# RMSNorm and matmul on one core: the loads of x move from SyncE's DMA queue to ScalarE's

## The chip, the cores and the metric

The kernel runs on one core of a Trainium2 chip. A core has five engines with instruction streams of their own: TensorE (PE, matrix products), VectorE (DVE), ScalarE (ACT), GpSimd (POOL) and SyncE (SP), which computes nothing here and issues transfers. Transfers between device memory and the core's SBUF are carried out by 16 DMA engines. SyncE and ScalarE each have a DMA queue; what one of them issues goes through its queue. The metric is the device time of one execution in microseconds (us), given as the median of many runs.

## The reference

x has 16 x 1024 rows (tokens) of 512 numbers, the weight is 512 x 768, all float32. Each row is divided by its root mean square, multiplied by gamma and then by the weight:

```
rms = sqrt(mean(x ** 2, axis=-1) + eps)
out = (x / rms * gamma) @ weight          # 16 x 1024 x 768, float32
```

## The kernel before

The 16384 rows are 128 tiles of 128 rows. Dividing by the rms commutes with the product, so the kernel multiplies the raw rows, in bfloat16, with a weight into which gamma has been folded once, and scales each row of the result by 1/rms while it leaves PSUM.

One step `j` of the main loop (lines 301 to 326) handles a pair of tiles, 2j and 2j + 1. The order of the instructions on each engine is the order of the program text; nothing reorders it. For a tile:

- A load brings x into a buffer of 16 tiles (`xt`, `xin` with two buffers, 32 KB per partition each). `load_until(2 * j + AHEAD)` with `AHEAD = 20` (line 302) issues the load of the next 16 tiles at the top of iterations 7, 15, 23, 31, 39 and 47 (tiles 32, 48, 64, 80, 96, 112). The first 16 tiles come as loads of 2, 2, 4 and 8 tiles; tiles 16 to 31 as one load of 16, all issued before the loop (lines 234 to 237), with the weights between.
- GpSimd casts x to bfloat16 (`xb`, line 94, a pair at a time, three pairs ahead). TensorE transposes it against an identity matrix (line 133) two pairs ahead, woven between the matmuls by `feeder`; VectorE copies the transposes out of PSUM (`xT`, line 140). The last four tiles of each 16 from tile 28 on are cast four at a time (`cast_quad`, line 158) and transposed by VectorE in blocks (line 172) instead.
- ScalarE squares x and sums each row (line 98, two pairs ahead), takes the root for four tiles at once (line 102); VectorE inverts it (line 104).
- TensorE makes eight matmuls (line 194) into one of three PSUM accumulators (`ops`). `finish_tile` scales the result into an output buffer: ScalarE for even tiles (line 176), VectorE for odd ones (line 178).
- The output buffer (`ot`) holds 8 tiles, and there are three of them. When 8 tiles are done, `store` (line 191) writes them out in one transfer of 3072 KB (two, two and four tiles, then four and four at the start, four and four at the end). A buffer is written again 24 tiles later, once its store has landed.

All loads of x and of the weights and all stores are issued by SyncE (lines 83, 191, 232), on one queue. So a load on that queue stands behind the stores issued before it. Four tiny transfers of a corner of x into an unused tile (`mark`, line 265) are issued at j = 30 and four more at j = 54. ScalarE issues one transfer, gamma, at the start (line 226).

In iteration j the order on ScalarE is: squares of tiles 2j + 4 and 2j + 5, in every second iteration a root, the scaling of tile 2j.

Of the kernel before, what the change touches and what calls it, by code (L numbers as in the profile page):

```python
# [18 lines left out]
def kernel(  # L19
# [8 lines left out]
    nc = tc.nc  # L28
    P = 128

    x = x.flatten_outer_dims()
    out = out.flatten_outer_dims()
# [4 lines left out]
    NP = NT // 2  # L37
    XG, OG = 16, 8
# [7 lines left out]
    def stretches(group, parts):  # L46
        first, size, i = {}, {}, 0
        for g in range(NT // group):
            for n in parts.get(g, [group]):
                for t in range(i, i + n):  # L50
                    first[t], size[t] = i, n
                i += n
        return first, size

    last = NT // OG - 1
    x_first, x_size = stretches(XG, {0: [2, 2, 4, 8]})
    o_first, o_size = stretches(OG, {0: [2, 2, 4], 1: [4, 4], last: [4, 4]})

    def rows(ap, i, n):
        base, t = x_first[i], x_size[i]  # L60
        return ap[base * P:(base + t) * P, :].rearrange("(p t) d -> p t d", t=t)[:, i - base:i - base + n, :]

    singles = ctx.enter_context(tc.tile_pool(name="singles", bufs=1))
# [11 lines left out]
    x_tiles, xb_tiles, tp_tiles, rstd_of, xT_tiles, o_tiles, norm_sums = {}, {}, {}, {}, {}, {}, {}  # L75

    def held(tiles, group, i, n=1):
        return tiles[i // group][:, i % group:i % group + n, :]

    def load(i):  # L80
        if i // XG not in x_tiles:
            x_tiles[i // XG] = xin.tile([P, XG, D], F32, name="xt")
        nc.sync.dma_start(out=held(x_tiles, XG, i, x_size[i]), in_=rows(x, i, x_size[i]))  # L83

    starts = [i for i in range(NT) if x_first[i] == i]

    def load_until(i):
        while starts and starts[0] < i:
            load(starts.pop(0))

    def cast(i, engine, n=1):
        if i // 2 not in xb_tiles:
            xb_tiles[i // 2] = xbp.tile([P, 2, D], BF16, name="xb")
        engine.tensor_copy(out=xb_tiles[i // 2][:, i % 2:i % 2 + n, :], in_=held(x_tiles, XG, i, n))  # L94
# [13 lines left out]
    def norms(i, n):  # L108
        ssq = stats.tile([P, 4], F32, name="ssq")
        for t in range(n):  # L110
            square(i + t, ssq[:, t:t + 1])
        root(i, n, ssq)
# [30 lines left out]
    def transpose_tile(i):  # L143
        for h in range(2):
            transpose_word(i // 2, i % 2, h)
        evac(i // 2, i % 2, 1)
# [6 lines left out]
    def quad_of(j):  # L153
        return j // 2 if (2 * j) % XG >= XG - 4 and 2 * j >= XG else None
# [14 lines left out]
    def move_quad(n):  # L169
        for _ in range(min(n, len(quad_moves))):  # L170
            dst, src = quad_moves.pop(0)
            nc.vector.transpose(out=dst, in_=src)  # L172

    def scale(engine, dst, src, r):
        if engine is nc.scalar:
            nc.scalar.mul(out=dst, in_=src, mul=r)  # L176
        else:
            nc.vector.tensor_single_scalar(out=dst, in_=src, scalar=r, op=mybir.AluOpType.mult)  # L178

    def accumulator():  # L180
        return opsum.tile([P, 2, WIDE], F32, name="ops").rearrange("p a b -> p (a b)")
# [16 lines left out]
    def matmuls(i, acc, ks, feed=None):  # L198
        for k in ks:
            matmul(i, k, acc, 0, WIDE)  # L200
            if feed:
                feed()
            matmul(i, k, acc, WIDE, O)

    def finish_tile(i, acc, engine):
        scale(engine, out_tile(i), acc[:, :O], rstd_of[i])
        store(i)


    def feeder(pairs, gaps, alone=False):  # L210
        queue = [(j, t, h) for j in pairs for t in range(2) for h in range(2)]
        calls = iter(gaps)

        def feed():
            for _ in range(next(calls)):
                j, t, h = queue.pop(0)
                transpose_word(j, t, h)
                if alone and h == 1:
                    evac(j, t, 1)
                elif (t, h) == (1, 1):  # L220
                    evac(j)
        return feed

    with tc.manual_schedule():
        g_row = singles.tile([2, P, 2], F32)
        nc.scalar.dma_start(out=g_row, in_=gamma.rearrange("(h w c) -> h w c", w=P, c=2))
        nc.scalar.preload_act_table(AF.Sqrt)  # L227
        wv = weight.rearrange("(h w c) o -> w h (c o)", w=P, c=2)
        w_f32 = singles.tile([P, K, O], F32)

        def load_weights(h):
            nc.sync.dma_start(out=w_f32[:, 2 * h:2 * h + 2, :].rearrange("p c o -> p (c o)"), in_=wv[:, h, :])  # L232

        load_until(2)
        load_weights(0)
        load_weights(1)
        load_until(2 * XG)

        for _ in range(20):
            nc.sync.drain()  # L240


        warm = singles.tile([P, WIDE], BF16)
        nc.vector.memset(warm, 0.0)
        eps_sb = singles.tile([P, 1], F32)
        nc.vector.memset(eps_sb, float(eps))  # L246
        ident_f = singles.tile([P, P], F32)
        make_identity(nc, ident_f)
        spare = accumulator()

        def warm_up(n):
            for _ in range(n):
                nc.tensor.matmul(out=spare[:, :WIDE], lhsT=warm[:, :P], rhs=warm, start=True, stop=True)  # L253

        w_bf = singles.tile([P, K, O], BF16)

        def weights(k, engine, lo=0, hi=O):
            scale(engine, w_bf[:, k, lo:hi], w_f32[:, k, lo:hi], g_sb[:, k % 2, k // 2:k // 2 + 1])


        probe = singles.tile([16, 16 * 64], F32)

        def mark(counts):
            for k in counts:
                nc.sync.dma_start(out=probe[:k, 64 * k:64 * k + 4 * k], in_=x[:k, :4 * k])

        warm_up(6)
        gp = tpsum.tile([P, 2, 2], F32, name="tp")
        for c in range(2):
            nc.tensor.transpose(out=gp[:, c, :], in_=g_row[:, :, c], identity=ident_f[:2, :2])  # L270
        g_sb = singles.tile([P, 2, 2], F32)
        nc.vector.tensor_copy(out=g_sb, in_=gp)  # L272
        cast(0, nc.gpsimd)
        cast(1, nc.gpsimd)
        cast(2, nc.gpsimd, 2)
        norms(0, 2)
        warm_up(4)
        transpose_tile(0)
        transpose_tile(1)
        warm_up(2)  # L280
        weights(0, nc.vector, 0, WIDE)
        weights(0, nc.vector, WIDE, O)
        weights(1, nc.scalar)
        acc = [accumulator() for _ in range(2)]
        for i in range(2):
            matmuls(i, acc[i], [0, 1])
        weights(2, nc.vector)
        weights(3, nc.scalar)
        norms(2, 2)
        cast(4, nc.gpsimd)  # L290
        cast(5, nc.gpsimd)
        matmuls(0, acc[0], [2, 3])
        finish_tile(0, acc[0], nc.scalar)
        matmuls(1, acc[1], [2, 3], feeder([1], [2, 2], alone=True))
        finish_tile(1, acc[1], nc.vector)
        cast(6, nc.gpsimd, 2)

        mid, one, two, both = ([0, 0, 1, 1, 0, 1, 1, 0], [1, 1, 0, 1, 1, 0, 0, 0], [1, 0, 1, 0, 1, 0, 1, 0],
                               [1, 1, 1, 1, 1, 1, 1, 1])
        marks = {NP // 2 - 2: (8, 10, 12, 14), NP - 10: (7, 9, 11, 13)}  # L300
        for j in range(1, NP):
            load_until(2 * j + AHEAD)
            if j + 3 < NP and quad_of(j + 3) is None:
                cast(2 * j + 6, nc.gpsimd, 2)
            if (2 * j + 2) % XG == 0 and 2 * j + 2 < NT:
                cast_quad((2 * j + 2 + XG - 4) // 4)
            elif 2 * j >= XG:
                move_quad(3)
            if j < 4:
                norms(2 * j + 2, 2)  # L310
            if 3 <= j < NP - 2:
                norms_by_four(j + 2)
            if j in marks:
                mark(marks[j])
            if j < 3:
                feed = feeder([j + 1], mid if j == 1 else one, alone=j == 1)
            elif j == 3:
                feed = feeder([4, 5], both)
            elif j + 2 < NP and quad_of(j + 2) is None:
                feed = feeder([j + 2], two)  # L320
            else:
                feed = None
            for i, engine in ((2 * j, nc.scalar), (2 * j + 1, nc.vector)):
                a = accumulator()
                matmuls(i, a, range(K), feed)
                finish_tile(i, a, engine)
# [35 lines left out]
```

## Time and profile before

| | |
|---|---|
| median of 14 runs | 210.65 us (210.41 to 212.64) |
| profiled execution: its own time / span | 210.8 us / 208.9 us |
| TensorE busy | 193.5 us (93% of the span) |
| VectorE, ScalarE, GpSimd busy | 151.0, 149.6, 64.3 us |
| packets on SyncE's queue | 85.48 MB, 96.8% of the time of 16 DMA engines |
| store of 8 tiles: issue to landing | 16.3 us (median of 13 issues) |
| load of 16 tiles: issue to landing | 21.3 us |
| last store issued / landed | 200.54 / 207.9 us |

The profile is of one execution. Its span goes from the first to the last instruction; the time of a run is about 1.9 us longer. In groups of instructions a line such as "L94 POOL CAST xb<-xt" names the source line, the engine, the operation and what is written from what. In a timeline the columns are the start in us from the span's start, the duration in us, then engine, line and operation, and in brackets the idle time before it and what ended that. An engine name with a "q" (SPq) is its instruction sequencer, which issues transfers. In a row of windows the columns are the stretch, its length, then busy us of each engine with the number of instructions (PE, weight loads, DVE, ACT, POOL), the granted clock of TensorE as a share, the mean busy share of the DMA engines, and the GB/s that they moved.

### The profile page before, as it was taken

To read this page: it belongs to the slowest core of one execution; us is meant where nothing else is said; L and a number is where in the kernel's file an instruction comes from. 1 tells how busy PE (TensorE), PEld (TensorE's weight loads), DVE (VectorE), ACT (ScalarE), POOL (GpSimd) and SP (SyncE) were. 2 spreads that over 40 slices of the span, in tenths; PEclk is the share of its full clock that TensorE was granted. 3 is DMA by queue.
4 is the path that set the end of the run, shared out by engine and by line. 5 is a ranking of instruction groups with operands and counts; after the bars stand their busy time and mean duration, and the time that the engine had idled before them with its cause. 6 is when DMAs were issued, how large, how long until landed. Compare 5 with 4: busy or idle time off the path is not lost.

```text
span 208.9 us, 3443 instructions
## 1 busy us (share of the span) xinstructions
PE 193.5 (93%) x1214; PEld 129.6 (62%) x1238; DVE 151.0 (72%) x270; ACT 149.6 (72%) x358; POOL 64.3 (31%) x65
## 2 busy tenths in 40 slices
PE   7799969999999999999999999999999989999910
PEld 2467746676666667666667666776666657666500
DVE  0465635999579966999579966998589965999410
ACT  4698758778787787778787787778787778778310
POOL 3247059004810193005810086002920059000000
PEclk9999999999999999999999999999999999999995
DMA  6999999999999899999999999999999999995994
GB/s 236 428 441 471 336 389 433 474 403 420 431 439 414 353 447 452 414 419 431 424 442 425 434 420 433 449 430 417 420 442 425 423 430 442 413 414 231 449 409 202
DMA packets 4941, 85.69 MB, mean 410 GB/s; under 512 B 698, under 2 KB 700, under 8 KB 1468
## 3 DMA queue, kind: packets, MB, share of 16 engines
q1 hardware_dynamic: 4920, 85.48, 96.8%
q8 instruction: 9, 0.15, 0.3%
q14 instruction: 8, 0.07, 0.1%
q10 hardware_dynamic: 4, 0.00, 0.0%
HBM read 35.14 MB, written 50.33 MB: 409 GB/s over the span
## 4 chain that ended last, share of the span: by engine, by line
PE 67%; DMA 24%; SPq 1%; POOL 1%; ACT 1%; issue 1%; DVE 0%; POOLq 0%
PE ops L194 60%; DMA xt<-in_x_dram 24%; PE tp L133 8%; POOL xb L94 1%; SPq L83 1%; ACT jk L98 1%; DVE ot L178 0%; ACT ot L176 0%; SPq L232 0%; POOLq L94 0%
## 5 line engine op out<-in xcount | busy, mean ns | idle before, releaser
L194 PE MATMUL ops<-w_bf,xT 128*128 128x256 bf16 (+1 forms) x783 | 146.5, 325 | 1.4 <-DVE w_bf L178 0.6
L194 PEld LDWEIGHTS <-xT 128*128 128x128 bf16 x800 | 78.3, 98 | 46.3 <-issue 0.8
L176 ACT ACTIVATE ot<-ops,rstd 128x768 f32<-128x768 f32 x64 | 57.7, 901 | 42.3 <-PE ops L194 41.9
L94 POOL CAST xb<-xt 128x1024 bf16<-128x1024 f32 (+1 forms) x52 | 51.1, 1010 | 112.7 <-DMA xt<-in_x_dram 104.2
L98 ACT ACTIVATE jk<-xt 128x512 bf16<-128x512 f32 x128 | 78.8, 620 | 3.4 <-DMA xt<-in_x_dram 3.4
L178 DVE TENSOR_SCALAR ot<-ops,rstd 128x768 f32<-128x768 f32 x64 | 64.6, 1010 | 9.5 <-PE ops L194 9.0
L133 PE MATMUL tp<-ident_f,xb 128*128 128x128 f32 x200 | 54.0, 274 | 2.9 <-POOL xb L94 2.9
L140 DVE COPY xT<-tp 128x1024 bf16<-128x1024 bf16 (+1 forms) x53 | 34.7, 657 | 26.2 <-PE tp L133 25.5
L172 DVE STREAM_TRANSPOSE xTq<-xq 32x256 f32<-32x256 f32 x112 | 48.7, 435 | 1.9
L194 PE MATMUL ops<-w_bf,xTq 128*128 128x256 bf16 (+1 forms) x217 | 42.5, 324 | 0.4
L133 PEld LDWEIGHTS tp<-ident_f,xb 128*128 128x128 f32 x200 | 28.2, 142 | 7.1 <-POOL xb L94 4.7
L194 PEld LDWEIGHTS <-xTq 128*128 128x128 bf16 x224 | 22.0, 98 | 12.4
L98 ACT ACTIVATION_READ_ACCUMULATOR jk<-xt 128x1 f32 x128 | 24.4, 191 | 0.0
L158 POOL CAST xq<-xt 128x2048 bf16<-128x2048 f32 x7 | 13.3, 1897 | 0.0
L104 DVE RECIPROCAL rstd<-rms 128x4 f32<-128x4 f32 (+1 forms) x35 | 6.1, 176 | 7.6 <-ACT rms L102 6.9
L102 ACT ACTIVATE rms<-ssq,eps_sb 128x4 f32<-128x4 f32 (+1 forms) x35 | 10.4, 297 | 1.1
L253 PE MATMUL ops<-warm 128*128 128x512 bf16 x12 | 5.2, 587 | 1.2 <-DVE eps_sb L246 1.2
L253 PEld LDWEIGHTS <-warm 128*128 128x128 bf16 x12 | 1.4, 128 | 2.9 <-issue 1.7
L176 ACT ACTIVATE w_bf<-w_f,g_sb 128x768 bf16<-128x768 f32 x2 | 1.9, 936 | 1.2 <-DMA w_f<-in_weight_dram 1.2
L272 DVE COPY g_sb<-tp 128x4 f32<-128x4 f32 x1 | 0.2, 163 | 3.2 <-PE tp L270 3.2
L227 ACT ACT_TABLE_LOAD x1 | 1.3, 1283 | 1.3 <-PEq L343 1.3
L178 DVE TENSOR_SCALAR w_bf<-w_f,g_sb 128x512 bf16<-128x512 f32 (+2 forms) x3 | 1.4, 482 | 0.3 <-DMA w_f<-in_weight_dram 0.3
(10 smaller groups left out, 1.9 us busy)
## 6 DMA issues: line engine op xcount, KB each, us to landing
out_dram<-ot SPq DMA_DIRECT2D x13, 3072.0 KB, 16.3
xt<-in_x_dram SPq DMA_DIRECT2D x7, 4096.0 KB, 21.3
out_dram<-ot SPq DMA_DIRECT2D x5, 1536.0 KB, 7.4
xt<-in_x_dram SPq DMA_DIRECT2D x1, 2048.0 KB
w_f<-in_weight_dram SPq DMA_DIRECT2D x2, 768.0 KB
out_dram<-ot SPq DMA_DIRECT2D x2, 768.0 KB, 16.0
xt<-in_x_dram SPq DMA_DIRECT2D x2, 512.0 KB, 3.4
xt<-in_x_dram SPq DMA_DIRECT2D x1, 1024.0 KB
```

Source lines behind the costliest of these rows:

```text
L94: engine.tensor_copy(out=xb_tiles[i // 2][:, i % 2:i % 2 + n, :], in_=held(x_tiles, XG, i, n))
L98: nc.scalar.activation(out=jk, in_=held(x_tiles, XG, i)[:, 0, :], func=AF.Square, accum_out=ssq)
L102: nc.scalar.activation(out=rms[:, :n], in_=ssq[:, :n], func=AF.Sqrt, scale=1.0 / D, bias=eps_sb)
L104: nc.vector.reciprocal(out=rstd[:, :n], in_=rms[:, :n])
L133: nc.tensor.transpose(out=tp_tiles[j][:, t, h, :], in_=words[:, lo:lo + P], identity=ident_f)
L140: nc.vector.tensor_copy(out=dst[:, t:t + n, :], in_=src[:, t:t + n, :])
L158: nc.gpsimd.tensor_copy(out=quads[q], in_=held(x_tiles, XG, 4 * q, 4))
L172: nc.vector.transpose(out=dst, in_=src)
L176: nc.scalar.mul(out=dst, in_=src, mul=r)
L178: nc.vector.tensor_single_scalar(out=dst, in_=src, scalar=r, op=mybir.AluOpType.mult)
L194: nc.tensor.matmul(out=acc[:, lo:hi], lhsT=xT_tiles[i // 2][:, i % 2, k // 2, :, k % 2], rhs=w_bf[:, k, lo:hi], start=(k == 0), stop=(k == ...
L253: nc.tensor.matmul(out=spare[:, :WIDE], lhsT=warm[:, :P], rhs=warm, start=True, stop=True)
```

## The change

Three things change. Tiles 16 to 31 are loaded in two transfers of eight tiles, one after the other on SyncE; the rows keep their place in the buffer. The loads from tile 32 on are issued by ScalarE, on its own queue, at the same place in the program text: the top of iterations 7, 15, ... 47. That is after the scaling of tile 2j - 2 and before the squares of tiles 2j + 4 and 2j + 5 in ScalarE's order. Stores stay with SyncE. The tiny transfers at j = 30 are left out; those at j = 54 take 12 to 15 partitions instead of 7, 9, 11 and 13. The orders on TensorE, VectorE and GpSimd are as they were.

```diff
-    x_first, x_size = stretches(XG, {0: [2, 2, 4, 8]})
+    x_first, x_size = stretches(XG, {0: [2, 2, 4, 8], 1: [8, 8]})
...
     def rows(ap, i, n):
-        base, t = x_first[i], x_size[i]
+        base, t = (x_first[i], x_size[i]) if i < XG else (i - i % XG, XG)
         return ap[base * P:(base + t) * P, :].rearrange("(p t) d -> p t d", t=t)[:, i - base:i - base + n, :]
...
     def load(i):
         if i // XG not in x_tiles:
             x_tiles[i // XG] = xin.tile([P, XG, D], F32, name="xt")
-        nc.sync.dma_start(out=held(x_tiles, XG, i, x_size[i]), in_=rows(x, i, x_size[i]))
+        queue = nc.sync if i < 2 * XG else nc.scalar
+        queue.dma_start(out=held(x_tiles, XG, i, x_size[i]), in_=rows(x, i, x_size[i]))
...
-        marks = {NP // 2 - 2: (8, 10, 12, 14), NP - 10: (7, 9, 11, 13)}
+        marks = {NP - 10: (12, 13, 14, 15)}
```

## The prediction

> **What bounds the kernel now.** I read the page first: the busy line of TensorE, the queue table and the slices.
>
> ```profile
> PE 193.5 (93%) x1214; PEld 129.6 (62%) x1238; DVE 151.0 (72%) x270; ACT 149.6 (72%) x358; POOL 64.3 (31%) x65
> DMA  6999999999999899999999999999999999995994
> q1 hardware_dynamic: 4920, 85.48, 96.8%
> ```
>
> TensorE is at 93% and SyncE's one DMA queue at 96.8%: two limits lie on top of each other. Which one ends last differs by stage, so I took windows, one for each repeat of a load and two stores, and one near the end.
>
> ```profile
> 83.10:107.40 24.30, 24.14 (x156) 16.51 (x158) 20.14 (x36) 18.46 (x45) 8.01 (x8) 1.00 1.01 432
> 107.40:131.70 24.30, 24.14 (x156) 16.52 (x158) 20.11 (x37) 19.02 (x46) 7.87 (x7) 1.00 1.01 431
> 188.00:192.00 4.00, 4.00 (x25) 2.49 (x25) 3.84 (x8) 3.60 (x10) 0.00 (x0) 1.00 0.46 197
> ```
>
> In mid-run the DMA engines are full (share 1.01) at 431 GB/s. Sixteen tiles move 4.19 MB in and 6.29 MB out, 10.49 MB, and so need 24.3 us: 9.7 us for the load, 7.3 us for each store. TensorE needs less: stores are issued on a beat of 23.42 us (119.56 to 142.97), with no TensorE gap. So the transfers fall 0.9 us further behind in every sixteen tiles. The casts on GpSimd show who pays; they start when a load lands.
>
> ```profile
> 28.43 3.01 POOL L94 CAST xb<-xt 128x1024 bf16<-128x1024 f32 x3 [7.62 <-DMA xt<-in_x_dram]
> 120.93 3.01 POOL L94 CAST xb<-xt 128x1024 bf16<-128x1024 f32 x3 [14.33 <-DMA xt<-in_x_dram]
> 145.14 3.02 POOL L94 CAST xb<-xt 128x1024 bf16<-128x1024 f32 x3 [15.11 <-DMA xt<-in_x_dram]
> 169.71 3.01 POOL L94 CAST xb<-xt 128x1024 bf16<-128x1024 f32 x3 [16.26 <-DMA xt<-in_x_dram]
> ```
>
> Landings are 24.2 to 24.6 us apart: the DMA beat, not TensorE's. TensorE itself waited for x twice:
>
> ```profile
> 29.52 0.33 PE L133 MATMUL tp<-ident_f,xb 128*128 128x128 f32 x1 [1.84 <-POOL xb L94]
> 170.80 0.33 PE L133 MATMUL tp<-ident_f,xb 128*128 128x128 f32 x1 [0.54 <-POOL xb L94]
> ```
>
> At 29.5 it lost 1.84 us to tiles 16 to 31, and at 170.8, when the margin of the loads was used up, 0.54. The end hangs on TensorE's place: the store of tiles 112 to 119 was issued at 190.57, when DMA was partly idle (share 0.46), and the last sixteen tiles' 6.29 MB then took 14.6 us plus fixed parts, to 207.9. Every microsecond that tile 119 moves, the end moves.
>
> **What the Trainium skill says.** "DMA: Bandwidth & Descriptors", section "Issuing engines are not separate DMA queues": transfers of all issuing engines run on the same 16 DMA engines, and a second issuer saves only issue time. The trace agrees as far as it can: 431 GB/s with one queue, share 1.01, leaves no idle engine for a second queue. Section "Queues, rings and completion order" of the same page: a DMA engine takes turns between the rings that have work, at packet granularity. No run here shows it, as only one ring carries x and out. Section "Where 436 GB/s comes from" puts the ceiling at 435 GB/s; the 431 measured is there already.
>
> **The split of tiles 16 to 31.** Bytes and order stay; one issue is added on SyncE (0.43 us, in the shadow of transfers queued ahead). The first half lands 2.1 MB / 431 GB/s = 4.9 us earlier, at about 23.4 instead of 28.3. TensorE wanted its transpose at 29.52 - 1.84 = 27.7, less a cast of 1.05: needed by 26.6. The second half lands as before, and is first wanted by the GpSimd cast of tiles 28 to 31, after three others; those moves on VectorE are spread over later pairs. Gain: 1.84 us in hand at 30 us.
>
> **What that gain meets.** Alone, I price it at nearly nothing: from 28 to 169 the queue is full and serves in order, so the load of tile 112 lands near 169.6 however early TensorE is, and the 0.54 us wait grows to about 2.4. The stall has moved 140 us, not gone.
>
> **The loads on ScalarE.** Six loads (tiles 32 to 112) leave SyncE's order. There each waited for ScalarE's squares of the buffer's last tiles (6.2 us in four waits). On ScalarE each stands at the top of iteration j = 7, 15, ... 47, behind the scaling of tile 2j - 2. For the last, before:
>
> ```profile
> 144.96 0.34 SPq L83 DMA_DIRECT2D xt<-in_x_dram  x1
> 148.18 0.90 ACT L176 ACTIVATE ot<-ops,rstd 128x768 f32<-128x768 f32 x1 [0.37 <-PE ops L194]
> 148.98 0.62 ACT L98 ACTIVATE jk<-xt 128x512 bf16<-128x512 f32 x1
> ```
>
> It would be issued at 149.0, 4.0 us later. Its semaphore wait on GpSimd is free (buffer last cast near 130). Behind it on ScalarE stand two squares, perhaps a root, and the scaling of tile 2j, for which TensorE's accumulator waits. Issue price: 0.34 us as SyncE pays here, 0.53 us as ScalarE's own gamma load (page start); I take 0.5, six times = 3 us of ScalarE, hidden in its gap before each scaling (0.37 to 0.92 us, 41.9 in all). Without that cover it is at most 3 us on the path.
>
> Against the later issue: no stores ahead of it. In order, load 112 took 24.6 us (144.96 to 169.6). Time to spare now: TensorE, unstalled, wants it landed by 170.26 - 1.05 - 0.15 = 169.05; from 149.0 that is 20.0 us, whatever the shift of both. What the load takes depends on how engines share, which the trace of before does not show. Fixed part: the first 512 KB load landed 3.4 us after issue, 1.2 of them bytes, so 2.2. The low end is an undisturbed load, 2.2 + 9.7 = 11.9 us. With stores always pending and packets in turn, a partition's load row is 32 KB against 24 KB of a store, so eight of each on an engine take 9.7 + 7.3 = 17.0: 19.2 in all, 0.8 inside the limit. With equal bytes, 2 x 9.7 + 2.2 = 21.6: 1.6 late. I take packets in turn, and keep both ends.
>
> **Where the debt goes then.** The 0.9 us deficit per sixteen tiles remains; if loads don't carry it, stores do. Store of tiles 80 to 87: issued 142.97, less 1.84 = 141.1. In order its packets moved from about 150 to 158 (packet records of the trace). Now the load of 112, entering at 149.0 - 1.84 + 1.2 = 148.4, takes turns with it: 150 + 17 = 167, plus about 0.5 to land. Its buffer is written again by tile 104, whose scaling ran at 166.19 on ScalarE, now 164.4: ScalarE waits up to 3 us. Three accumulators let TensorE run two tiles (2.8 us) past tile 104, against a normal evacuation of 0.9, so 1.9 us is covered; 0.2 to 1.2 us reaches TensorE. The same pattern stands at tiles 88 and 72, so three such waits at 0.8: 2.4 us. Between these, VectorE's scaling of the odd tile waits too, with no more loss.
>
> **The marks.** Four tiny loads at j = 30 go (2.85 us of SyncE), four at j = 54 change shape. In the old order they delayed the issue of load 80 to 99.49, but its landing kept the 24.3 us beat: nothing. Without the queue's cover they would have cost 2 us on that load.
>
> **Sum**, against the profiled execution (span 208.9, its own time 210.8, median of the runs 210.65): first stall -1.84, second -0.54, store waits +2.4, ScalarE issue 0, marks 0: 0.0. Forecast **210.7**; this case's own range is 209.2 to 212.2 (waits of 0.3 to 1.3 us each).
>
> **Rivals.** *Slower: loads late on their ring.* If an engine shares by bytes, or a load in company is otherwise slowed beyond 20.0 us, TensorE waits at pairs 14, 22, ... 54. This renews itself: a late load delays ScalarE, which issues the next one later. Five loads at 0.9 us (the DMA beat itself) to 1.6 cost 4.5 to 8, less the 2.4 saved: +2.1 to +5.6; I take +4.3, **215**. It decides as soon as a load takes over 20.0 us from its issue; my own case is only 0.8 from that, and the 4.0 us later issue speaks for it.
>
> *Faster: both stalls go and stores pay nothing.* If a load, once begun, mostly goes through (near 12 us) and stores land within about 25 us of issue, the 2.4 us stay: **208.3**. For it: DMA idles near 190, so in bytes the room is there. Against: the deficit must be carried by someone until 165.
>
> *It does nothing*: loads on time, waits only at the end; counted with the forecast.
>
> **How the numbers follow.** Forecast case 0.50; loads late 0.38; faster 0.12. I count a half per cent (1.05 us) as about what a measurement tells from no change. From the first case 0.08 falls faster, 0.30 same, 0.12 slower; the second is slower; the third is faster. So faster 0.20, same 0.30, slower 0.50: the likeliest single case is no change, but the slow side is heavier. The range, 208.6 to 215.6, takes the first case whole, most of the slow one and half of the fast one.
>
> **What would show it.** Right: no TensorE wait near 29; casts of tile 16 near 24; loads landing 17 to 20 us after issue on ScalarE; ScalarE's scalings of tiles 72, 88 or 104 waiting for a DMA from out, and stores at 22 to 27 us to landing instead of 16.3. Wrong towards slow: TensorE waiting for casts at every sixteenth tile, landings over 20 us, stores quick. Wrong towards fast: neither wait. The whole reckoning fails if two rings move more or fewer bytes than 431 GB/s.

## The result, and the profile after

The changed kernel is slower: 213.06 us (median of 10 runs, 212.64 to 214.30) against 210.73 us for the kernel before beside it. The ratio is 1.0107, with a 95% interval of 1.0078 to 1.0135, so 2.25 us, from 1.6 to 2.8. The forecast was 210.7, no change. The time lies in the stated range, but that range spans nearly all three cases, and the waits are those of the rival that I gave 0.38: the mechanism of my own case did not come true.

The profiled execution took 214.26 us, with a span of 212.5, so it is one of the longer ones: its first store was issued 0.6 us later than before (13.47 against 12.88), which the profiles of its variants E2, E3, E4 and E6 below do not repeat (12.74 to 12.96). From the page of the kernel after: the busy line, the slices of the DMA engines, the two queues, and the shares of the chain that ended last.

```profile
PE 194.5 (92%) x1214; PEld 129.5 (61%) x1238; DVE 150.9 (71%) x270; ACT 149.9 (71%) x358; POOL 64.3 (30%) x65
...
DMA  6999999999999999999999999999999999873994
...
q1 hardware_dynamic: 4140, 60.31, 67.4%
q10 hardware_dynamic: 868, 25.17, 27.9%
...
DMA 55%; PE 36%; POOL 3%; issue 1%; SPq 1%; DVE 0%; POOLq 0%; ACT 0%
```

Busy times are within 1 us of those of before; the 85.5 MB are now split over two queues. In the chain, the share of DMA has gone from 24% to 55%: the way back from the end now runs mostly through loads of x. The gap in the DMA slices near the end (5994 before) is wider (873994). The timeline of TensorE shows who waits:

```profile
76.81 0.33 PE L134 MATMUL tp<-ident_f,xb 128*128 128x128 f32 x1 [1.71 <-POOL xb L95]
101.53 0.33 PE L134 MATMUL tp<-ident_f,xb 128*128 128x128 f32 x1 [1.09 <-POOL xb L95]
125.91 0.33 PE L134 MATMUL tp<-ident_f,xb 128*128 128x128 f32 x1 [0.74 <-POOL xb L95]
149.82 0.33 PE L134 MATMUL tp<-ident_f,xb 128*128 128x128 f32 x1 [0.27 <-POOL xb L95]
174.31 0.33 PE L134 MATMUL tp<-ident_f,xb 128*128 128x128 f32 x1 [0.85 <-POOL xb L95]
```

Five waits for x, one in each sixteen tiles from the load of tile 48 on, 4.66 us together; before there were two, 1.84 and 0.54. The difference is 2.3 us. Each such stop costs some 0.2 us more than its wait: in the sixteen tiles of the first, 25.35 us lie between ScalarE's scalings of tiles 32 and 48, where an unstalled stretch takes 23.42 and the wait is 1.71. Counted so, the stops come to 5.8 us after and 2.8 before. That is 2.9 of the 3.5 us by which this execution is longer than the profiled one of before, and its late start is the other 0.6; in the medians the loss is 2.25. The wait at 29 us is gone, as the split was to bring. No engine waited for a store: the 13 stores of 8 tiles landed 18.4 us after issue (16.3 before).

The casts on GpSimd again mark the landings. Ahead of them, the issues of the loads of tiles 48 and 64 on ScalarE's sequencer:

```profile
53.02 0.33 ACTq L84 DMA_DIRECT2D xt<-in_x_dram  x1
78.37 0.34 ACTq L84 DMA_DIRECT2D xt<-in_x_dram  x1
```

```profile
22.28 2.03 POOL L95 CAST xb<-xt 128x1024 bf16<-128x1024 f32 x2 [0.89 <-DMA xt<-in_x_dram]
48.63 3.01 POOL L95 CAST xb<-xt 128x1024 bf16<-128x1024 f32 x3 [13.77 <-DMA xt<-in_x_dram]
75.71 3.01 POOL L95 CAST xb<-xt 128x1024 bf16<-128x1024 f32 x3 [17.43 <-DMA xt<-in_x_dram]
100.44 3.01 POOL L95 CAST xb<-xt 128x1024 bf16<-128x1024 f32 x3 [16.81 <-DMA xt<-in_x_dram]
124.81 3.02 POOL L95 CAST xb<-xt 128x1024 bf16<-128x1024 f32 x3 [16.46 <-DMA xt<-in_x_dram]
148.72 3.02 POOL L95 CAST xb<-xt 128x1024 bf16<-128x1024 f32 x3 [15.99 <-DMA xt<-in_x_dram]
173.22 3.01 POOL L95 CAST xb<-xt 128x1024 bf16<-128x1024 f32 x3 [16.58 <-DMA xt<-in_x_dram]
```

Set beside the kernel before, this is the heart of the case (us from the span's start; "takes" is from issue to the cast):

| load of tile | 32 | 48 | 64 | 80 | 96 | 112 |
|---|---|---|---|---|---|---|
| before: cast starts | 50.09 | 72.38 | 96.62 | 120.93 | 145.14 | 169.71 |
| after: cast starts | 48.63 | 75.71 | 100.44 | 124.81 | 148.72 | 173.22 |
| after is later by | -1.5 | 3.3 | 3.8 | 3.9 | 3.6 | 3.5 |
| before: takes | 20.8 | 21.1 | 21.9 | 21.4 | 23.6 | 24.8 |
| after: takes | 19.0 | 22.7 | 22.1 | 21.7 | 21.2 | 21.8 |

After is late once, at the load of 48, and then keeps the same beat as before: 97.3 and 97.5 us from the load of 48 to that of 112, 24.3 to 24.4 for each sixteen tiles. TensorE alone would need 23.42. The difference, 0.9 us in every sixteen tiles, is what I call the debt below. Before, the load *takes longer and longer*, 21.1 to 24.8 us (that of tile 80 is out of line because the marks delayed its issue), and that growth swallows most of the debt, because SyncE issues early. After, every load from tile 48 on takes about 22 us, nothing grows, and TensorE itself waits for the difference.

The rate of the DMA engines did not change. Windows of the kernel after, one in mid-run and two near the end (columns as before: stretch, length, busy us of the engines, clock, DMA share, GB/s):

```profile
104.40:128.80 24.40, 23.51 (x152) 15.83 (x154) 19.28 (x35) 18.30 (x46) 7.89 (x8) 1.00 1.00 430
188.00:192.00 4.00, 3.95 (x27) 2.81 (x27) 3.88 (x9) 3.06 (x7) 0.00 (x0) 1.00 0.49 209
192.00:196.00 4.00, 4.00 (x27) 2.44 (x26) 3.85 (x8) 3.60 (x10) 0.00 (x0) 1.00 0.45 190
```

Two queues move 430 GB/s where one moved 431. But after the last load the engines run half empty for 8 us instead of 4. The trace lists every packet with its queue, start, length and size. From these packet records, the idle time of an engine between 180 us and the last store packet is 6.4 us after and 3.2 us before (mean of the 16), and that packet ends 3.2 us later (210.62 against 207.44). The bytes are the same and the rate is the same, so the 3.2 us of extra idling is the longer run, seen from the side of DMA: TensorE came late to the last tiles, and the stores that should fill the engines did not yet exist.

**What one load now consists of.** For the load of tile 112 the packet records give 151.38 (issue) to 154.81 (first packet), 3.4 us; to 171.69 (last packet), 16.9 us; to 173.07 (landed), 1.4 us; together 21.7. The middle is what I had worked out with packets in turn (17.0). Where load rows and store rows alternate, the load's packets start 2.12 us apart: 1.21 for a load row of 32 KB, 0.91 for a store row of 24 KB, one of each. The two ends I had put at 2.2; they are 4.8. That the sum lies at the 21.6 that I had for sharing by equal bytes is chance. At the far end the short packet that reports the landing comes 0.91 us after the last load row, the length of one store row (mostly 0.46 in E6, where store rows are half as long). The near end is 3.4 to 3.9 us in all six loads of this kernel, and 3.5 to 4.0 in E6, so the row size of the stores does not set it. On idle engines it was 0.9 us (the store at 194.08, on SyncE's queue). What the busy engines do in these microseconds stays open. In order, on one queue, the last packet of the same load ended at 169.08 and the cast began at 169.71.

### The profile page after: what moved, and what is told of

Same layout as the page of the kernel before. It is cut to its first block, busy times and chain, and to the rows that moved or that the text cites. A ratio compares the mean times of both kernels' runs of the same rounds, so it can differ in the third digit from the quotient of the medians.

```text
span 212.5 us, 3432 instructions
## 1 busy us (share of the span) xinstructions
PE 194.5 (92%) x1214; PEld 129.5 (61%) x1238; DVE 150.9 (71%) x270; ACT 149.9 (71%) x358; POOL 64.3 (30%) x65
## 4 chain that ended last, share of the span: by engine, by line
DMA 55%; PE 36%; POOL 3%; issue 1%; SPq 1%; DVE 0%; POOLq 0%; ACT 0%
DMA xt<-in_x_dram 55%; PE ops L195 31%; PE tp L134 5%; POOL xb L95 3%; SPq L233 0%; DVE ot L179 0%; SPq L84 0%; POOLq L95 0%; ACT ot L177 0%
## 5 line engine op out<-in xcount | busy, mean ns | idle before, releaser
L99 ACT ACTIVATION_READ_ACCUMULATOR jk<-xt 128x1 f32 x128 | 24.4, 190 | 0.0
## 6 DMA issues: line engine op xcount, KB each, us to landing
out_dram<-ot SPq DMA_DIRECT2D x13, 3072.0 KB, 18.4
xt<-in_x_dram ACTq DMA_DIRECT2D x6, 4096.0 KB, 21.6
```

Of the source, the lines that this page charges most:

```text
L99: nc.scalar.activation(out=jk, in_=held(x_tiles, XG, i)[:, 0, :], func=AF.Square, accum_out=ssq)
```

## The experiments

The theory at this point: a load that shares the engines in turn with stores takes 21.7 us against 20.0 to spare, because of its two ends. The rivals changed as the runs came in; each is in the expectations.

### E1: the split alone

```diff
 # the kernel before
-    x_first, x_size = stretches(XG, {0: [2, 2, 4, 8]})
+    x_first, x_size = stretches(XG, {0: [2, 2, 4, 8], 1: [8, 8]})
```

> Of the change only the split of tiles 16 to 31; all transfers stay on SyncE's one queue. Theory (the transfers are behind in mid-run, so a gain at the start is paid back at the last load): TensorE does not wait near 29 us, the load of tile 112 still lands at 169 to 170, TensorE's wait there grows from 0.54 to 2 us or more, time 210.2 to 211.0. Rival (a gain at the start is kept to the end): 208.5 to 209.2.

Measured: 210.57 us, ratio 0.9988 (0.9971 to 1.0004). From its timelines, TensorE's wait for tile 96, the cast of tile 112 and TensorE's wait for it:

```profile
145.65 0.33 PE L133 MATMUL tp<-ident_f,xb 128*128 128x128 f32 x1 [0.61 <-POOL xb L94]
169.24 3.01 POOL L94 CAST xb<-xt 128x1024 bf16<-128x1024 f32 x3 [16.78 <-DMA xt<-in_x_dram]
170.34 0.33 PE L133 MATMUL tp<-ident_f,xb 128*128 128x128 f32 x1 [1.06 <-POOL xb L94]
```

The wait at 29 us is gone, the load of 112 lands where it did (169.24 against 169.71), and waits for x stand near the end instead: 0.61 and 1.06 us, 1.7 together, in place of 0.54. So of the 1.84 us gained at 30 us, 1.1 is given back by 170, less than I had expected at the last load (2 or more). What is left is too little for the time to show.

### E2: the loads on ScalarE without the split

```diff
 # the kernel after
-    x_first, x_size = stretches(XG, {0: [2, 2, 4, 8], 1: [8, 8]})
+    x_first, x_size = stretches(XG, {0: [2, 2, 4, 8]})
```

> The changed kernel without the split: tiles 16 to 31 in one transfer again. Theory (loads that take 21.6 us from issue against some 20 to spare set the pace from tile 48 on): TensorE waits 1.8 us near 29 again, which lets the transfers catch up, so the first wait at tile 48 is smaller by about as much; time 212.5 to 213.8, the same as changed within 0.5. Rival (each wait adds): 214.5 to 215.

Measured: 214.62 us (four runs), ratio 1.0173 (1.0099 to 1.0247). From its summary of waits (us in total, times, longest):

```profile
PE tp L134 <- POOL xb L95: 6.1, 5, 2.1
```

One of the five, 0.70, belongs to the start and stands in the kernel after too (0.70 at 11.0). TensorE waited 2.14 at 29.7 and still 1.82 at 78.6, so the early wait did not make the one at tile 48 smaller, as I had expected; the median lies in the rival's range. Its interval overlaps that of the kernel after, so how much the split is worth with two queues is not settled. That the loss is there without the split is settled.

### E3: the loads on ScalarE issued earlier

```diff
 # the kernel after, in the loop over j
-            load_until(2 * j + AHEAD)
...
             norms_by_four(j + 2)
+            load_until(2 * j + AHEAD + 4)
```

The load of tile 48 is issued at 49.18 instead of 53.02: about where SyncE issues it in E1 (49.29).

> The changed kernel with ScalarE's loads issued two iterations earlier in its order, just behind the squares of the last tiles of the buffer that they overwrite: some 4 to 6 us earlier. Theory (the late place in ScalarE's order is what makes the loads late): issue to landing stays 21 to 22.5 us, TensorE's waits for x fall from 4.7 us to under 0.7, stores land later (20 to 26 us), time 209.0 to 211.0. Rival A (the bytes of sixteen tiles, 24.3 us, set the pace whatever the order): TensorE waits as much, for stores or for x, 212.5 to 213.5. Rival B (two rings in turn, or issuing from ScalarE, cost as such): 212.5 to 213.5, with waits for x gone.

Measured: 213.74 us (four runs), ratio 1.0145 (1.0101 to 1.0189). Its summary of waits:

```profile
ACT ot L177 <- DMA out_dram<-ot: 13.3, 5, 3.5
PE ops L195 <- ACT ot L177: 4.6, 4, 1.5
DVE ot L179 <- DMA out_dram<-ot: 4.2, 4, 1.4
```

The waits for x are gone from the main loop, and no time came back: ScalarE now waits for output buffers whose stores have not landed (in mid-run they take 22 to 28 us), and TensorE for ScalarE, 4.6 us in four waits where it was 4.66 in five. My theory, that the late place of the issue makes the loss, fell; in kind it is rival A, at a time a little above its range. The loss belongs to the two queues together: in turn both the load and the stores beside it end late, and whichever is needed first is waited for.

### E4: stores half as long

```diff
 # the kernel after: stores of four tiles up to tile 111
-    o_first, o_size = stretches(OG, {0: [2, 2, 4], 1: [4, 4], last: [4, 4]})
+    o_first, o_size = stretches(OG, {0: [2, 2, 4], last: [4, 4], **{g: [4, 4] for g in range(1, last - 1)}})
```

> The changed kernel with stores of four tiles (rows of 12 KB) up to tile 111 in place of eight; loads at the same late place. Theory (engines take packets in turn, one of each ring): a load packet of 32 KB stands against 12 KB, a load takes 16 to 18.5 us from issue, TensorE's waits for x vanish, time 209 to 211. Rival (engines share by bytes): a load still takes 21 to 22.5 us and the time is 212.5 to 213.5.

Measured: 213.45 us (four runs), ratio 1.0110 (1.0059 to 1.0162): the time expected, 209 to 211, was missed. The profile is of the longest run (217.64 us), so only the order of things is read from it. Loads were quicker, 18.8 to 20.2 us (E6, with stores of the same size, has 18.6 to 20.1), as turns by rows demand when the other side's rows are 12 KB, and the waits for x went. The debt turned up at the stores again:

```profile
ACT ot L177 <- DMA out_dram<-ot: 14.5, 4, 5.0
PE ops L195 <- ACT ot L177: 6.6, 4, 3.0
```

### E5: the marks alone

```diff
 # the kernel before
-        marks = {NP // 2 - 2: (8, 10, 12, 14), NP - 10: (7, 9, 11, 13)}
+        marks = {NP - 10: (12, 13, 14, 15)}
```

> The kernel before with the change's marks alone (none at j = 30, other sizes at j = 54). Theory, as in the prediction: the marks only delay an issue that stands in a full queue, so 210.3 to 211.1 us, ratio within 0.3% of 1. Rival: they are part of the loss or of a gain; then over 0.6 us to either side.

Measured: 210.67 us against 211.00 beside it, ratio 0.9993 (0.9958 to 1.0027). As expected, no part of the loss that 0.7 us of noise would let through.

### E6: more room for the stores, two queues

If the output buffers are what E3 and E4 ran into, more of them should take the waits away. Four of eight tiles do not fit, seven of four do.

```diff
 # the kernel after
-    XG, OG = 16, 8
+    XG, OG = 16, 4
...
-    o_first, o_size = stretches(OG, {0: [2, 2, 4], 1: [4, 4], last: [4, 4]})
+    o_first, o_size = stretches(OG, {0: [2, 2]})
...
-    outp = ctx.enter_context(tc.tile_pool(name="out", bufs=3))
+    outp = ctx.enter_context(tc.tile_pool(name="out", bufs=7))
```

> The kernel after with output buffers and stores of four tiles, seven of them (28 tiles, where three of eight hold 24). A buffer is written again 24 tiles (35 us) after its store is issued instead of 16 (23.4 us). Theory now: with two queues in turn both transfers that run together finish late, and TensorE loses time because one of the two is needed before that; loads against stores of four took 18.8 to 20.2 us and stores 22 to 28. With 35 us to spare the waits for the output buffers go, the waits for x stay gone, and the time is 206.5 to 208.7 us. Rival: the bytes set the pace (24.3 to 24.6 us for sixteen tiles) whatever the buffers; loads are late again or stores pass 35 us, and the time stays at 212 to 214.

Measured: 211.59 us, ratio 1.0021 (0.9998 to 1.0044). From its windows, two in mid-run and three at the end:

```profile
120.00:145.00 25.00, 25.00 (x164) 16.98 (x163) 20.03 (x36) 19.73 (x48) 9.31 (x10) 1.00 1.00 422
145.00:170.00 25.00, 25.00 (x164) 16.98 (x163) 20.13 (x36) 19.34 (x48) 9.31 (x9) 1.00 1.01 424
...
196.00:198.00 2.00, 0.68 (x5) 0.20 (x2) 1.02 (x1) 0.32 (x1) 0.00 (x0) 1.00 1.01 430
198.00:200.00 2.00, 0.00 (x0) 0.00 (x0) 0.00 (x0) 0.00 (x0) 0.00 (x0) 1.00 1.04 442
...
204.00:206.00 2.00, 0.00 (x0) 0.00 (x0) 0.00 (x0) 0.00 (x0) 0.00 (x0) 0.50 0.26 111
```

TensorE is busy 25.00 of 25.00 us: with 35 us instead of 23.4 for a store, every wait of size is gone, though stores take up to 31 us (128.57 to 159.41). So the waits were indeed a matter of how much lateness the buffers can hold. But the time did not follow. TensorE is through before 198 us, DMA is not: it has its whole debt left. With store rows of 12 KB DMA moves 422 to 426 GB/s, where the same stretches of the kernel before have 427 to 431, and at the end some engines finish some six us after the others (the share falls below 1 from 200 us on; the last packet ends at 209.0). With TensorE free of waits the transfers are the bound, and my 206.5 to 208.7 was too low because I had priced only TensorE's side.

### E7: the same buffers, one queue

The edit of E6, on the kernel before.

> The kernel before with the same seven output buffers and stores of four tiles, all on SyncE's one queue. Theory: in order the debt falls on the loads, not on the stores, so more room in the output buffers does nothing for the waits at 29 and 170 us (2.4 us together); only the end is filled better by smaller stores, some 1 to 2 us: 208.5 to 209.8 us, and not faster than the same buffers with two queues. Rival: smaller stores cost the DMA engines more or the order helps as much: 210.5 or more, or below 208.

Measured: 212.92 us, ratio 1.0081 (1.0055 to 1.0106). Expected was 208.5 to 209.8, a clear miss; the rival (smaller stores cost the DMA engines more) had 210.5 or more. One of its windows:

```profile
120.00:145.00 25.00, 24.28 (x159) 16.20 (x157) 19.89 (x35) 18.69 (x47) 7.86 (x7) 1.00 1.00 425
```

In order the debt sits on the loads, and the lower rate of small rows adds to it: 10.49 MB at 425 GB/s is 24.7 us for sixteen tiles instead of 24.3, by my estimate some 2 us over the run. TensorE waited 6.7 us for x in five waits of the main loop. The same buffers that helped with two queues (ratio 1.0021 for 1.0107) hurt with one, because each order puts the debt in another place.

### E8: a finer end on one queue

```diff
 # E1's kernel
-    o_first, o_size = stretches(OG, {0: [2, 2, 4], 1: [4, 4], last: [4, 4]})
+    o_first, o_size = stretches(OG, {0: [2, 2, 4], 1: [4, 4], last - 1: [4, 4], last: [4, 2, 2]})
```

> The kernel before with tiles 16 to 31 in two loads, and at the end stores of 4, 4, 4, 2 and 2 tiles instead of 8, 4 and 4. In the kernel before DMA idles for 2.4 us between 184 and 192 us, before the last drain. Theory: these bytes move earlier and the last store is half as long, so 208.3 to 209.3 us. Rival: the end is set by the last tile of TensorE and the fixed part of the last store, not by the drain: 210.0 to 210.7.

Measured: 210.62 us against 211.00 beside it, ratio 0.9965 (0.9943 to 0.9987). The idle stretch was filled, but the time gained only 0.7 us of the 2.4, part of which may be E1's split (0.25, within its noise); this is the rival's range. Its windows:

```profile
188.00:192.00 4.00, 4.00 (x26) 2.49 (x25) 3.83 (x8) 3.60 (x10) 0.00 (x0) 1.00 0.92 393
...
204.00:206.00 2.00, 0.00 (x0) 0.00 (x0) 0.00 (x0) 0.00 (x0) 0.00 (x0) 0.50 0.20 83
206.00:208.00 2.00, 0.00 (x0) 0.00 (x0) 0.00 (x0) 0.00 (x0) 0.00 (x0) 0.50 0.06 25
```

From 188 to 192 the share rose from 0.46 to 0.92, and by 204 most engines are done (0.20, where the kernel before has 0.96 from 204 to 206); the last one finishes at 207.6. So a few engines end the run, not the bytes on average; why these are behind stays open. This kernel is faster than both the kernel before and the kernel after; E9's stands level with it.

### E9 and E10: one load on ScalarE

If the loss is a debt that can be paid only once, one load on the second queue should cost nothing when the later ones go in order.

```diff
 # E1's kernel; 48 in E9, 112 in E10
-        nc.sync.dma_start(out=held(x_tiles, XG, i, x_size[i]), in_=rows(x, i, x_size[i]))
+        queue = nc.scalar if i == 48 else nc.sync
+        queue.dma_start(out=held(x_tiles, XG, i, x_size[i]), in_=rows(x, i, x_size[i]))
```

> The kernel before with tiles 16 to 31 in two loads, and the load of tiles 48 to 63 alone issued by ScalarE on its queue; all others stay with SyncE. Theory now (the debt): DMA is full until 180 us and falls about 0.93 us further behind TensorE in every sixteen tiles; a wait of TensorE pays some of it, and what is paid early is not paid again. So the load of 48 lands 21 to 23 us after its issue, TensorE waits 1.2 to 1.8 us near 76 us, the waits near 145 and 170 us (0.61 and 1.06 with one queue) shrink to 0 to 0.5, and the time is 210.3 to 211.1 us. Rival (each load that is late on its ring adds its wait): the waits at the end stay, and the time is 211.8 to 212.5.

Measured in E9: 210.39 us, ratio 0.9967 (0.9947 to 0.9986), inside the theory's 210.3 to 211.1. From its timelines:

```profile
74.76 3.01 POOL L95 CAST xb<-xt 128x1024 bf16<-128x1024 f32 x3 [15.91 <-DMA xt<-in_x_dram]
95.87 3.02 POOL L95 CAST xb<-xt 128x1024 bf16<-128x1024 f32 x3 [13.19 <-DMA xt<-in_x_dram]
```

The load of 48 lands 3.3 us later than in E1 (71.42), just the lateness of the kernel after. The next load, in order again, lands at 95.87 against 95.66 in E1: I take it that the stores that were let ahead are done by then, so that it finds a shorter queue. The wait near 76 us was only 0.19, since this execution had waited 0.95 for the load of 32; the 1.2 to 1.8 that I gave it is a miss, and the total, 1.8 us in three waits of the main loop, is near E1's 1.7.

> The kernel before with tiles 16 to 31 in two loads, and the load of tiles 112 to 127 alone issued by ScalarE on its queue. Theory now: in order that load already takes 26 us from SyncE's place, with the debt of the five before it; on ScalarE it is issued near 147.5 and lands 21.7 us later, near 169.3, as in order (169.1), so TensorE waits 1.0 to 1.8 us for it and the time is 210.4 to 211.4 us. The second queue costs only when it is used for load after load, since it takes away the time that loads have in hand before the debt builds up. Rival (store packets let ahead of the last load are what costs: 37.9 MB of stores done when it ends instead of 36.8): it lands at 171 to 172, and the time is 212.4 to 213.4.

Measured in E10: 211.84 us, ratio 1.0036 (1.0015 to 1.0057), between theory (up to 211.4) and rival (from 212.4), and in neither. Against E1 that is about 1 us lost (1.0036 to 0.9988, the intervals apart), so one load on the second queue can cost too, where no later load in order follows. Its load landed near 170.8 (expected 169.3), and from its timelines on ScalarE and TensorE:

```profile
169.93 0.90 ACT L177 ACTIVATE ot<-ops,rstd 128x768 f32<-128x768 f32 x1 [3.87 <-DMA out_dram<-ot]
```

```profile
170.88 1.46 PE L195 MATMUL ops<-w_bf,xT 128*128 128x512 bf16 x8 [1.89 <-ACT ot L177]
```

That is the wait which my prediction had put into the changed kernel: tile 104's scaling stands behind the store of tiles 80 to 87, issued at 141.89 and sharing the engines with the load. Here TensorE had waited only 1.8 us for x before it (3.8 in the kernel after), so there is less lateness elsewhere to hide it. The store bytes done when the last load ended (37.0 MB) are near E1's 36.8, so the rival's cause, store bytes let ahead of the last load, is not what cost here.

## Where the prediction held and where it failed, step by step

**What bounds the kernel: right.** TensorE and DMA both full, 0.9 us of debt per sixteen tiles at 431 GB/s. In the kernel after, the four beats from the load of 48 to that of 112 take 97.5 us where TensorE alone would need 93.7, and the four later stops, waits and after-costs together, make just these 3.8 us.

**The split: right in place, near in worth.** Casts of tile 16 at 22.28, no wait near 29, and alone no gain that the time shows (E1): 1.7 us of waits for x near the end against my 2.4.

**The issue on ScalarE and the marks: right.** 0.33 to 0.37 us each instead of my 0.5, hidden; marks nothing (E5).

**The step that failed is the time of a load in company, in the part on the loads on ScalarE.** The bytes in turn, 17.0 us, were right (16.9). The fixed part was taken from a load that ran with idle engines: 2.2 us, where the loaded engines gave 3.4 before and 1.4 behind (tile 112). So 19.2 became 21.7, beyond the 20.0 from which, as I had written, the slower rival decides. My margin of 0.8 us rested on a figure from the wrong condition.

**Where the debt goes: the mechanism exists, not in this kernel.** The stores never blocked a buffer after the change; TensorE already stood for x, so it came late to the buffers. Where the loads are made early enough (E3), or one load meets a TensorE that was held up less (E10), the waits appear as described: 3.87 us on ScalarE for my "up to 3", 1.89 on TensorE for my 0.2 to 1.2. So this term was too small as well: with the loads in time, E3 has four waits of 4.6 us together where I had put three of 0.8, or 2.4. A right figure for the load alone would still have left the sum some 2 us short. I had written that the 0.9 us of debt per sixteen tiles remains, and charged about half of it.

**The rival that came true was too steep.** It had five loads at 0.9 to 1.6 us and took the upper half, +4.3. It came at +2.25, near its lower end: after the first wait of 1.71 they fell to 0.27 to 1.09. A late load does delay the next issue, but it also lets the DMA engines catch up, so the waits follow the DMA beat.

**The faster rival** needed a load near 12 us; none came below 17.

What I had not seen is why the old order is better at equal bytes: in order a load can be issued early and grow older without harm, and the stores ahead of it end early (16.3 us after issue). Shared in turn, neither ends early: 18.4 us for the stores of the kernel after, 22 to 28 in E3. E1, E3, E6, E9 and E10 show the parts of that; that no other order of the two queues would do better is not shown.

## What to carry to other kernels

With the DMA engines full for most of the run, the second queue added no bytes per second here (430 GB/s against 431) and changed only who ends late, so ask which buffers can hold the lateness before moving a load. Take the latency of a transfer from one that ran in the same company: both ends of it, from issue to first packet (0.9 to 1.1 us on idle engines, 3.4 to 3.9 here) and from last packet to landing (0.6 in order, 1.4 beside stores), grew on busy engines. A stall that goes in a stage with a full queue can turn up at the next place where the debt falls due, and one experiment like E1 tells it for a small price.

## What the runs showed of the hardware that I had not expected

- Two queues with work took turns, one row each: load packets mostly 2.12 us apart, 1.21 + 0.91, and 1.67 with 12 KB rows on the other side (E6). The Trainium skill, "DMA: Bandwidth & Descriptors", section "Queues, rings and completion order", has turns by packets that hold some 9 to 17 descriptors; here the turn was a single record of 12, 24 or 32 KB; of how many descriptors a record consists, the trace does not show.
- From issue to first packet a load waited 3.4 to 3.9 us on engines with stores pending, against 1.1 us for the run's first load on idle ones. With store rows half as long it was no shorter (3.5 to 4.0, E6).
- In stretches of 25 us between 70 and 170 us, the kernels with store rows of 12 KB (E6, E7) moved 421 to 427 GB/s, those with 24 KB (before, after) 426 to 434. Single rows show the same (medians): 0.46 us for 12 KB, 0.912 for 24 KB, 1.213 for 32 KB, or 427, 431 and 432 GB/s for 16 engines. I estimate that this 1% costs some 2 us where DMA is the bound (E7).
- The 16 engines do not end together: some six us lay between the first and the last in E6, where TensorE's end left full queues behind. Why they are uneven stays open.
